# Block 2's experts: all blocks of slots go through one weight piece at a time, with a branch and a load per piece instead of per matrix

## The chip, the cores and the metric

The kernel runs on one core of one Trainium2 chip. The metric is the device time of one launch in microseconds (us). In the profile PE is TensorE's matmuls and PEld its weight loads, DVE is VectorE, ACT is ScalarE, POOL is GpSimd and SP is SyncE, which here only issues transfers; a small q behind a name (PEldq, SPq) means the engine's sequencer, which runs branches, waits and register instructions.

## What is computed

Two blocks of a small network over 512 tokens of 1024 features: attention or recurrence first, then in each block a layer of experts. The change is in the experts of block 2 alone: 32 experts, of which each token goes through 4. From the reference, cut:

```python
def moe_ffn(h, router_w, router_b, w1, b1, w2, b2):
    ...
    logits = (xt @ router_w + router_b).astype(jnp.float32)
    top_val, top_idx = lax.top_k(logits, TOP_K_2)
    gates = jax.nn.softmax(top_val, axis=-1)
    ...
    def run_block(args):
        toks, e = args
        hb = x_pad[toks] @ w1[e] + b1[e]
        g_part = jnp.minimum(hb[..., ::2], SWIGLU_LIMIT)
        u_part = jnp.clip(hb[..., 1::2], -SWIGLU_LIMIT, SWIGLU_LIMIT)
        act = g_part * jax.nn.sigmoid(SWIGLU_ALPHA * g_part) * (u_part + 1)
        return act @ w2[e] + b2[e]
    ...
    out = jnp.zeros((t + 1, shp[-1]), xt.dtype).at[slot_tok].add(y_slots)[:t]
```

w1 of an expert is 1024 x 2048, w2 is 1024 x 1024, in 32-bit floats.

## The kernel before

How many tokens an expert has is only known when the kernel runs; `slots()` works it out and writes it to `cnt`. An expert's slots are cut in four blocks: A is slots 0 to 63, B 64 to 95, C 96 to 127, D 128 to 191. A always runs; B, C and D stand in nested branches on the count n (`If(n > 64)`, `If(n > 96)`, `If(n > 128)`). `ways` says how many column groups of the matmul array a block is spread over: 2 for A and D (matmuls of 64 slots), 4 for B and C (32 slots).

The weights of an expert come in 12 pieces of 1 MB, 8 of w1 and 4 of w2, into a ring of 17 buffers, all by SP's queue in the order of use (`load2w`). A load into a buffer waits until PE has used the piece that was there, and SP issues its loads one after the other.

`moe2` writes the order out by hand (`manual_schedule`). For each expert e: `hidden(e)`, the first product (`hidden2`, matmuls L2637, bias L2642, then on DVE and ACT the activation in L2647 to L2654); `rows(e + 2)`, the gathers of tokens on POOL; the transposes of the next expert's rows, X[e + 1] (L1652); loads; `output(e - 1)`, the second product of the expert before (`output2`, L2668, bias L2671, scaling on DVE into `yy` in L2674, added into the result by a scatter on POOL); loads; the transposes of expert e's result, A[e] (L1652). In `hidden` and `output` there is one `If(n > 64)` each (L2729, L2749); inside, block A's product is done first and then B's, with C and D in nested Ifs (L2731, L2735, L2737 and L2751, L2755, L2757), and an `Else` holds a second copy of block A's product for the experts that have no more. Within a matrix a block goes through all of its pieces before the next block begins, so that the pieces of w1 are let go one by one only during the last block.

The sums of the products lie in PSUM: a pool `ps2` of two pairs of banks for first products, and a pool `ps` of four banks, in turns, for transposes, second products and the matmuls of `slots()`.

Of the kernel before, what the change touches and what calls it, by code (L numbers as in the profile page):

```python
# [85 lines left out]
class Parts:  # L86
    """A float32 operand as the sum of two parts that the tensor engine carries in one pass each."""
# [7 lines left out]
class Pieces:  # L95
    """Blocks in two tiles of four."""
# [7 lines left out]
class Net:  # L104
# [18 lines left out]
    def constants(self):  # L123
# [20 lines left out]
        # additive masks: NEG where the column is before the row / after the row / not after it  # L144
# [9 lines left out]
        # partition numbers  # L154
# [28 lines left out]
    def rsqrt(self, in_, n, scale, eps, name, P=128):  # L183
        """(scale * in_ + eps) ** -0.5 by Newton's method, from the exponent's half."""
# [18 lines left out]
    def vectors(self):  # L203
        """The small vectors: their loads; those of the modulations' inputs as columns; the others."""
# [29 lines left out]
        # silu(c) as padded stationary operands  # L234
# [9 lines left out]
        # biases of the modulations whose vectors are wanted as columns  # L244
# [10 lines left out]
    def parts(self, x, hi, lo):  # L255
        """x as two parts: the rounded one, and what is left."""
# [4 lines left out]
    def mm(self, out, l, r, start, stop):  # L261
        """A matrix product; of operands in parts without the product of their small parts, which are below float32's last place."""
# [7 lines left out]
    def load2(self, src, kk, pool):  # L270
        """A block of weights [kk * 128, 1024 / kk]."""
# [4 lines left out]
    def split2(self, raw, kk, pool=None):  # L276
        """Its parts, in a piece of the ring."""
# [5 lines left out]
    def piece(self, src, ncol, kk=KD, pool=None):  # L283
        """A block of weights [kk * 128, ncol] as [128, kk, ncol]."""
# [12 lines left out]
    def norm_T(self, x, nt, A, B, hT, pool):  # L297
        """hT [128, 8, nt * 128] = (rmsnorm(x) * A + B) transposed."""
# [50 lines left out]
    def projections(self, pace):  # L349
# [3 lines left out]
        # the products by weights: their pieces in the ring, ahead of their parts, ahead of their use  # L353
# [46 lines left out]
        # the first modulation, norm, and what the others want of small inputs  # L400
# [188 lines left out]
    def mods(self, pace):  # L589
        """Both modulations, by two steps a chunk of 512: the first four chunks of each as columns of shifts and of  # L590
        (1 + scale) * norm, the others as a row in DRAM."""
# [11 lines left out]
        for c in range(24):  # L603
# [7 lines left out]
            # partial sums in rows 0, 32, 64, 96 (and 1, 33, ..)  # L611
# [54 lines left out]
    def delta(self, pace):  # L666
        """The gated delta rule, by steps; chunks of a tile of tokens."""
# [9 lines left out]
        # sums of squares of the heads, each in the rows that its factors take  # L677
# [11 lines left out]
        # selectors of the rows of factors, for the channels of a pair of heads  # L689
# [20 lines left out]
        # decays, rates  # L710
# [25 lines left out]
        # factors of q and k in rows: 32 * pair + 10 * part + 2 * kind + head of the pair  # L736
# [30 lines left out]
        # in three bfloat16 parts, which add up to the whole  # L767
# [34 lines left out]
        # token-major: values times rates, keys times decays to the chunk's end  # L802
# [3 lines left out]
        def to_tokens(src, t, fac):  # L806
            # in place: the block of a pair and a tile, channels by tokens, becomes tokens by channels
# [14 lines left out]
        # products of keys and queries within the chunks, with their decays  # L822
# [56 lines left out]
        # inverses of the unit lower triangles: diagonal blocks of 32 by substitution, one per partition  # L879
# [15 lines left out]
        # the transposed inverses take the place of the triangles, block by block; inverses of the blocks of 64, and  # L895
        # the products on the way, side by side
# [69 lines left out]
        # the chunks in turn  # L966
# [61 lines left out]
    def finish(self, pace):  # L1028
        """The outputs of the delta rule's chunks, normed and gated, transposed in the place of the values."""
# [42 lines left out]
    def softplus(self, out, a, b, shape, name):  # L1072
        """out = softplus(a + b)"""
# [9 lines left out]
    def attention(self, pace):  # L1083
        """Sliding-window attention, by steps; its outputs, transposed, in the place of the queries."""
        nc, I, sm, m, t2, ident = self.nc, self.I, self.sm, self.m, self.t2, self.ident
        bank = lambda: self.ps.tile([128, 512], FT, name="ps")
        # rotary angles
# [40 lines left out]
        # norms of the heads: of the queries [tile, 8], of the keys [tile, 2]  # L1128
# [15 lines left out]
        def rope(v, w, r, c, s, shape, ro):  # L1144
            # ro = the rotation of v * w * r by the angles of cosine c and sine s
# [31 lines left out]
        for t in range(NT):  # L1177
            # heads j and j + 4, of the two groups, side by side
# [104 lines left out]
    def out1(self, pace):  # L1283
        """x + gate * (mixed @ w_out) by tiles of tokens, kept in DRAM; by steps."""
# [38 lines left out]
    def norms1(self, pace):  # L1323
        """Norm, modulation and logits of the tiles that out1 is done with."""
# [17 lines left out]
    def norm_tile(self, x, A, B, t, i, h, hT, lg, hold=lambda **n: None):  # L1342
        """rmsnorm(x) * A + B of a tile of tokens: rows to DRAM for the experts; its logits; by steps."""
# [28 lines left out]
    def logits_init(self, pool, parts, n):  # L1372
        """Weights and biases of a router; parts: (w, b, columns)."""
# [11 lines left out]
    def dram_scratch(self):  # L1385
        """Rows of tokens for the experts, what their outputs are added to; spare rows are 512 to 639."""
# [5 lines left out]
        self.xe = [self.dp.tile([S + 128, D], FT, name=f"xe{i}") for i in range(1)]    # outputs of experts in turn in block 1  # L1392
        # numbers of experts, also less 64, halves and quarters
# [16 lines left out]
    def fill_scratch(self, z):  # L1410
        """First contents of the scratch; z: room for 512 words."""
# [9 lines left out]
    def selectors(self):  # L1421
        """Of the heads, by six, in the rows that block 2's decays are made of."""
# [9 lines left out]
    def windows(self):  # L1432
        """One over the sizes of block 2's pooling windows."""
# [10 lines left out]
    def biases(self, src, out):  # L1444
        """The biases of block 2's experts in DRAM as three bfloat16 parts, which add up to the whole."""
# [12 lines left out]
    def argmax(self, l, n, ix, last=False):  # L1458
        """Maximum over the last axis of l [128, 4, n], the one-hot of its first place, and that place less 64 in ix."""
# [29 lines left out]
            # the logits of the chosen group  # L1489
# [19 lines left out]
    def slot_consts(self):  # L1509
        """Numbers of slots, of the spare rows that empty ones take, and of tokens."""  # L1510
# [10 lines left out]
    def slots(self, i, hots):  # L1521
        """Tokens and gates of the first 192 slots of each expert, by blocks of slots; counts per expert."""
# [6 lines left out]
        # ranks of the tokens of an expert, and counts, also as a column  # L1529
# [16 lines left out]
        for k in range(K):  # L1546
# [3 lines left out]
            # the choice's experts times token and gate, and its slots  # L1550
# [24 lines left out]
        # by blocks, each slot as often as its row has pieces  # L1575
# [17 lines left out]
    def table(self, i, K):  # L1593
        """All slots in DRAM: row slot * 32 + expert has the token and its gate."""
# [22 lines left out]
    def mt(self, n, name, bufs):  # L1617
        """Room for n words; within the loop over further slots all pieces take turns in one ring."""
# [1237 lines left out]
```

## Time and profile before

| | us |
|---|---|
| median of 3 runs | 2909.01 |
| runs | 2908.73 to 2913.5 |
| profiled execution, span | 2899.8 |
| PE busy in it | 2242.4 |
| DVE busy in it | 841.4 |

The time of a run is some microseconds longer than the span of a profile, which begins with the first recorded instruction and ends with the last. The experts of block 2 lie in the second half of the span: expert 0's first transposes are at 1594.59 us, and the last product ends at 2870.3 us.

### The profile page before, as it was taken

Reading aid. Unit: us, or ns where it says so; the run is one execution under the profiler, and the core shown is the slowest. Engines: PE = TensorE matmul, PEld = TensorE weight load, DVE = VectorE, ACT = ScalarE, POOL = GpSimd, SP = SyncE. Lnnn points to the kernel's source line nnn. Section 1 sums busy time; section 2 is a strip of 40 time slices with the busy share of each in tenths; the row PEclk is TensorE's granted clock in tenths of the full one; section 3 lists DMA queues with packets and bytes.
Section 4 is the critical chain, followed back from the end, with each engine's and each line's share of the span. In section 5 each row is a group of like instructions: output and inputs, shape, how many; then the busy total and the mean of one; then the engine's idle time right before and its main releaser. Section 6 shows DMA issues by size and latency. Waiting matters only on the chain. (4 is left out here: it accounts for less than half of the span.)

```text
span 2899.8 us, 38736 instructions
## 1 busy us (share of the span) xinstructions
PE 2242.4 (77%) x14872; PEld 1270.8 (44%) x14911; DVE 841.4 (29%) x1743; ACT 551.1 (19%) x1049; POOL 511.7 (18%) x581
## 2 busy tenths in 40 slices
PE   6799698656775538999996877788688787787775
PEld 4566465534544327777685322233223232232222
DVE  3355734311121115666567111110111110110111
ACT  3343311201111016555431000000000000000000
POOL 2333011123331110233214010101101010001000
PEclk9899888678997769999997899899889898898987
DMA  7645424578787743222146988889878689999883
GB/s 266 241 159 176 160 95 167 166 240 260 234 233 247 241 147 92 72 59 65 58 142 228 356 334 334 343 320 361 329 292 313 270 333 358 366 365 366 337 311 103
DMA packets 262355, 691.54 MB, mean 238 GB/s; under 512 B 20199, under 2 KB 135514, under 8 KB 229176
## 3 DMA queue, kind: packets, MB, share of 16 engines
q1 hardware_dynamic: 230936, 614.19, 56.8%
q0 software_dynamic: 26480, 58.03, 7.9%
q10 hardware_dynamic: 4528, 13.63, 1.2%
q8 instruction: 283, 4.64, 0.7%
q14 instruction: 128, 1.05, 0.1%
HBM read 647.23 MB, written 38.57 MB: 237 GB/s over the span
## 5 line engine op out<-in xcount | busy, mean ns | idle before, releaser
L2637 PE MATMUL ps<-w,xT 128*64 128x512 f32 (+1 forms) x3136 | 623.0, 628 | 133.6 <-issue 121.8
L2637 PEld LDWEIGHTS ps<-w,xT 128*64 128x64 f32 (+1 forms) x3136 | 210.3, 136 | 518.0 <-issue 511.7
L2668 PE MATMUL ps<-w,aT 128*64 128x512 f32 (+1 forms) x2048 | 303.3, 507 | 69.4 <-issue 55.8
L1641 POOL DMA_INDIRECT xd<-yy,ix x49 | 77.6, 1583 | 1033.6 <-DVE yy L2674 918.4
L2647 DVE TENSOR_SCALAR gt<-ps 128x512 f32<-128x512 f32 (+1 forms) x49 | 29.6, 604 | 786.3 <-PE ps L2642 761.5
L2668 PEld LDWEIGHTS ps<-w,aT 128*64 128x64 f32 (+1 forms) x2048 | 118.4, 128 | 234.4 <-issue 212.7
L2652 ACT ACTIVATE sg<-gt 128x512 f32<-128x512 f32 (+1 forms) x49 | 27.5, 560 | 765.0 <-DVE gt L2647 765.0
L2674 DVE SCALAR_TENSOR_TENSOR yy<-ps,ga,gate 128x512 f32<-128x512 f32 (+1 forms) x49 | 32.5, 663 | 341.1 <-PE ps L2671 317.4
L1626 POOL DMA_INDIRECT gath<-hd,ix x94 | 93.0, 989 | 179.0 <-issue 46.6
L1667 PE MATMUL ps<-w,xA 128*32 128x128 f32 x1248 | 63.6, 370 | 73.7 <-issue 48.9
L266 PE MATMUL pf<-w,hh 128*128 128x256 f32 (+1 forms) x288 | 100.0, 347 | 2.0 <-ACT hh L257 2.0
L1654 ACT ACTIVATE aT<-ps 128x512 f32<-128x512 f32 (+1 forms) x48 | 24.9, 525 | 392.7 <-PE ps L1652 391.9
L267 PE MATMUL pf<-w,hh 128*128 128x256 f32 (+1 forms) x288 | 93.5, 324 | 0.0
L1667 PEld LDWEIGHTS ps<-w,xA 128*32 128x32 f32 x1248 | 53.6, 151 | 83.9 <-issue 83.2
L1672 DVE TENSOR_TENSOR act<-act,ps 128x64 f32<-128x64 f32 (+1 forms) x45 | 10.4, 230 | 261.0 <-ACT act L1671 236.7
L2019 PE MATMUL pf<-hc,w 128*128 128x256 f32 x256 | 75.8, 447 | 10.0 <-issue 6.0
L266 PE MATMUL pf<-b,b 128*128 128x512 f32 (+2 forms) x224 | 81.1, 362 | 0.0
L266 PE MATMUL pf<-hh,w 128*128 128x512 f32 x192 | 80.4, 419 | 0.0
L268 PE MATMUL pf<-b,b 128*128 128x512 f32 (+2 forms) x224 | 78.1, 349 | 0.5 <-DVE b L258 0.5
L267 PE MATMUL pf<-b,b 128*128 128x512 f32 (+2 forms) x224 | 78.2, 349 | 0.0
L1652 PE MATMUL ps<-ident,gath 128*128 128x128 f32 x266 | 49.3, 300 | 36.5 <-DVE aTA L1689 12.0
L258 DVE TENSOR_TENSOR w<-raw,w 128x1024 fp32r<-128x1024 f32 x52 | 69.0, 1347 | 26.7 <-ACT w L257 26.7
(714 smaller groups left out, 3665.9 us busy)
## 6 DMA issues: line engine op xcount, KB each, us to landing
w<-in_w_dram SPq DMA_DIRECT2D x378, 1024.0 KB
w<-in_w_ada_dram SPq DMA_DIRECT2D x24, 1024.0 KB
w<-in_w_mod_dram SPq DMA_DIRECT2D x24, 1024.0 KB
w<-in_w_down_dram SPq DMA_DIRECT2D x20, 1024.0 KB
w<-in_w_gate_dram SPq DMA_DIRECT2D x37, 512.0 KB
w<-in_w_up_dram SPq DMA_DIRECT2D x37, 512.0 KB
raw<-in_w_in_dram SPq DMA_DIRECT2D x36, 512.0 KB
b<-in_w_gate_dram SPq DMA_DIRECT2D x25, 512.0 KB
```

What stands on the lines that cost most here:

```text
L258: self.nc.vector.tensor_sub(lo, x, hi)
L266: self.nc.tensor.matmul(out, l.hi, r.hi, start=start, stop=False)
L267: self.nc.tensor.matmul(out, l.hi, r.lo, start=False, stop=False)
L268: self.nc.tensor.matmul(out, l.lo, r.hi, start=False, stop=stop)
L1626: nc.gpsimd.indirect_dma_start(out=g, out_offset=None, in_=self.hd[i].rearrange("t (a d) -> (t a) d", a=ways), in_offset=bass.IndirectOffs ...
L1641: self.nc.gpsimd.indirect_dma_start(out=x.rearrange("t (a d) -> (t a) d", a=ways), out_offset=bass.IndirectOffsetOnAxis(ap=ix, axis=0), in ...
L1652: nc.tensor.transpose(p[:, 128 * c:128 * c + 128], g[:, 128 * c:128 * c + 128], self.ident)
L1667: nc.tensor.matmul(p[n * q:n * q + n, 0:2 * f], xT[:, c, n * h:n * h + n], w[:, :, f * q:f * q + f], start=(k == 0), stop=(k == KD - 1))
L2019: nc.tensor.matmul(ps, w[:, k, c0:c0 + 128], hc[:, k], start=(k == 0), stop=(k == KD - 1))
L2637: nc.tensor.matmul(pp[n * j:n * j + n, b], xT[:, c, n * q:n * q + n], w[:, f0:f0 + 512], start=(k == 0), stop=False)
L2668: nc.tensor.matmul(p[n * q:n * q + n, :nd], aT[:, 2 * b + i, n * j:n * j + n], w[:, k % 2, nd * q:nd * q + nd], start=(k == 0), stop=False)
L2674: nc.vector.scalar_tensor_tensor(y, p[:, :nd], ga, self.gates[ways], op0=OP.mult, op1=OP.mult)
```

## The change

`hidden2` and `output2` are cut into a function for one piece of a matrix (`first2`, `second2`) and one for what follows the product (`act2`, `add2`). `hidden(e)` goes over the 8 pieces of w1; at each it runs block A's matmuls and then, in nested branches, those of B, C and D on the same piece, and then SP's load into a buffer is issued (`load`). `output(e)` does the same with the 4 pieces of w2. The `Else` copies are gone. All blocks of an expert are open at once, so the PSUM pools become `ps` with two banks and three named pairs: `h2` for A, `h4` for B and C, `h3` for D. `output` puts the sums of A, B and C into `h3` too, and D's into a bank of `ps`. The transposes of B, C and D move to `inputs` and `results`, with branches of their own, and each of these functions reads the count itself. The loop for more than 192 slots (`further`) uses the new functions, but isn't run with this data.

```diff
-        self.banks("o", 4)
+        self.banks("o", 2, 3)
...
-        def hidden(e):
-            w1 = [W[e, i] for i in range(8)]
-            n = N[e] = nc.values_load(self.cnt[0:1, e:e + 1], engines=self.four, min_val=0, max_val=S)
-            u = U[e] = [self.mt(512, "ut2", 1)]
-            g = G[e]
-            with tc.If(n > 64) as few:
-                x = [self.xpose(g[1], "xT4", 2)]
-                with tc.If(n > 96):
-                    x.append(self.xpose(g[2], "xT4", 2))
-                self.hidden2(X[e], 2, e, w1, 1, u[0])
-                u.append(self.hidden2(x[0], 4, e, w1, 4))
-                with tc.If(n > 96):
-                    u.append(self.hidden2(x[1], 4, e, w1, 4))
-                    with tc.If(n > 128):
-                        self.mp = mq
-                        u.append(self.hidden2(self.xpose(g[3], "xT2"), 2, e, w1, 2))
-            self.mp = mp
-            with few.Else():
-                self.hidden2(X[e], 2, e, w1, 1, u[0])
...
+        def beyond(n, f):
+            with tc.If(n > 64):
+                f(1)
+                with tc.If(n > 96):
+                    f(2)
+                    with tc.If(n > 128):
+                        self.mp = mq
+                        f(3)
+            self.mp = mp
...
+        def inputs(e):
+            X[e] = [self.xpose(G[e][0], "xT2")]
+            beyond(count(e, T.PE, T.Activation), lambda i: X[e].append(self.xpose(G[e][i], ("xT4", "xT4", "xT2")[i - 1], 2 if i < 3 else 1)))
...
+        def hidden(e):
+            n = N[e] = count(e, T.PE)
+            x = X.pop(e)
+            bc = pair("h4")
+            p = [pair("h2"), bc[:, 0:1], bc[:, 1:2], pair("h3")]
+            for k in range(KD):
+                f = lambda i: self.first2(p[i], x[i], ways[i], e, k, W[e, k])
+                f(0)
+                beyond(n, f)
+                load(12 * e + k + 18 - 4 * (e > 0))
+            u = U[e] = [self.act2(p[0], 2, 1)]
+            beyond(count(e, T.DVE, T.Activation), lambda i: u.append(self.act2(p[i], ways[i], 4 if i < 3 else 1)))
+
+        def output(e):
+            n, a = N.pop(e), A.pop(e)
+            U.pop(e)
+            es_ = slice(e, e + 1)
+            o = pair("h3")
+            o3 = self.ps.tile([128, 512], FT, name="ps")
+            p = [o[:, 0], o[:, 1, 0:256], o[:, 1, 256:512], o3]
+            for i in range(4):
+                f = lambda b: self.second2(p[b], a[b], ways[b], e, i, W[e, 8 + i], b != 2)
+                f(0)
+                beyond(n, f)
+                load(12 * e + i + 34)
+            f = lambda b: self.add2(p[b], self.blocks[b][0][:, es_], self.blocks[b][1][:, es_], ways[b])
+            f(0)
+            beyond(count(e, T.DVE, T.Pool), f)
...
```

The order of the instructions shows what this moves on PE. First, two pieces of block A's first product on PE, in the `Else` of L2729 before (`w_` is a buffer of the ring, `xT2` A's transposed rows, DMAHW a load's semaphore):

```order
L2637 MATMUL ps2_21834<-w_21032,xT2_21606 64x512 [waits DMAHW1_49]
L2637 MATMUL ps2_21834<-w_21032,xT2_21606 64x512 x3
L2637 MATMUL ps2_21834<-w_21034,xT2_21606 64x512 [waits DMAHW2_49]
L2637 MATMUL ps2_21834<-w_21034,xT2_21606 64x512 x3
L2637 MATMUL ps2_21834<-w_21036,xT2_21606 64x512 [waits DMAHW4_49]
L2637 MATMUL ps2_21834<-w_21036,xT2_21606 64x512 x3
```

The same place on PE after the change, one piece and the start of the next; the last unconditional branches, with a wait on PE's own semaphore (PE_49), are the arms that run when a block isn't there:

```order
L2634 MATMUL h2_22002<-w_21038,xT2_21920 64x512 [waits DMAHW6_49]
L2634 MATMUL h2_22002<-w_21038,xT2_21920 64x512 x3
L2736 COMPARE_AND_BRANCH
L2634 MATMUL h4_22001<-w_21038,xT4_21937 32x512 [waits DVE_49]
...
L2634 MATMUL h3_22003<-w_21038,xT2_21951 64x512 x3
L2740 UNCONDITIONAL_BRANCH
L2740 UNCONDITIONAL_BRANCH [waits PE_49]
L2738 UNCONDITIONAL_BRANCH [waits PE_49]
L2736 UNCONDITIONAL_BRANCH [waits PE_49]
L2634 MATMUL h2_22002<-w_21359,xT2_21920 64x512 [waits DMAHW7_49]
```

Between two pieces of A there was nothing but the wait for the next load; now there are a branch, the code of three other blocks, and an arm that waits for PE itself.

Second, where the second product of an expert begins on PE, before (in the If; `aT2` is A's transposed result):

```order
L2751 UNCONDITIONAL_BRANCH [waits PE_49]
L2668 MATMUL ps_22243<-w_21618,aT2_21927 64x512 [waits DMAHW4_49,PE_49,Activation_49]
L2668 MATMUL ps_22243<-w_21618,aT2_21927 64x512 x3
L2668 MATMUL ps_22243<-w_21906,aT2_21927 64x512 [waits DMAHW5_49]
L2668 MATMUL ps_22243<-w_21906,aT2_21927 64x512 x3
```

And after:

```order
L2736 UNCONDITIONAL_BRANCH [waits PE_49]
L2671 MATMUL h3_22293<-w_21649,aT2_21958 64x512 [waits DMAHW1_49,DVE_49,PE_49]
L2671 MATMUL h3_22293<-w_21649,aT2_21958 64x512 x3
L2736 COMPARE_AND_BRANCH
L2671 MATMUL h3_22293<-w_21649,aT4_21975 32x256 x8
```

The first matmul waited for the load and for ACT; it now waits for the load and for DVE (DVE_49), since its sums go to the pair h3.

## Rows read from the trace of the kernel before

**Rows 1.** Windows, experts of block 2; columns: busy us by engine, clock, DMA share

```profile
core 0: us, PE busy (x) PEld busy (x) DVE busy (x) ACT busy (x) POOL busy (x), PEclk, DMA share, GB/s
1594.60:2870.40 1275.80, 1010.18 (x5870) 383.09 (x5870) 145.61 (x244) 76.86 (x148) 122.12 (x95) 0.90 0.84 325
2650.00:2700.00 50.00, 33.45 (x148) 12.67 (x148) 5.64 (x9) 3.01 (x6) 6.18 (x5) 0.88 1.00 395
```

**Rows 2.** Waits of PE in 1594.6:2870.4; waiting line, releaser, total us, times, longest

```profile
PE ps L2637 <- issue: 121.8, 20, 7.2
PE ps L2668 <- issue: 55.8, 15, 7.5
PE ps L1652 <- DVE yy L2674: 19.5, 20, 1.0
PE ps L1652 <- PEq L2755: 11.5, 4, 3.3
PE ps L1652 <- ACT sg L2652: 10.0, 9, 1.3
PE ps L2637 <- DMA w<-in_w_dram: 6.7, 1, 6.7
```

**Rows 3.** Single lines' sequencer instructions: count, ns min/median/max, first and last start

```profile
L2729 PEldq COMPARE_BRANCH  x32: 65/6050/6871, 1595.3 to 2815.9; - x32
...
L2751 PEldq COMPARE_BRANCH  x16: 70/202/228, 1647.0 to 2841.0; - x16
...
L2749 ACTq EVENT_SEMAPHORE  x20: 17/17/17, 1689.0 to 2857.9; - x20
...
L2731 PEldq EVENT_SEMAPHORE  x8: 51/51/51, 1596.2 to 2728.9; - x8
...
L2737 PEldq EVENT_SEMAPHORE  x3: 51/51/51, 1962.6 to 2799.3; - x3
...
L2726 PEldq TENSOR_LOAD <-cnt x32: 300/306/321, 1594.6 to 2815.2; - x32
```

**Rows 4.** Timeline of PE; start, us, line, tiles, count, idle time before and releaser

```profile
1711.37 15.80 PE L2637 MATMUL ps<-w,xT 128*64 128x512 f32 x64 [6.32 <-issue]
...
1730.02 7.09 PE L2668 MATMUL ps<-w,aT 128*64 128x512 f32 x32 [0.30 <-PEq L2751]
...
1742.72 0.41 PE L1652 MATMUL ps<-ident,gath 128*128 128x128 f32 x2 [0.33 <-PE ps L1652]
1743.28 13.95 PE L2637 MATMUL ps<-w,xT 128*64 128x512 f32 x64
```

**Rows 5.** Windows behind a gap, and within a first product that has none ahead

```profile
1711.60:1715.00 3.40, 3.40 (x10) 1.04 (x10) 0.00 (x0) 0.00 (x0) 0.00 (x0) 0.50 1.05 390
...
1743.30:1757.20 13.90, 13.90 (x66) 5.65 (x68) 0.00 (x0) 0.31 (x1) 2.59 (x2) 1.00 0.89 332
```

**Rows 6.** PE by line and form in 1594.6:2870.4; busy us, mean ns, idle before

```profile
L2637 PE MATMUL ps<-w,xT 128*64 128x512 f32 x2112 | 509.9, 645 | 133.6 <-issue 121.8 <-DMA w<-in_w_dram 6.7 <-PEq L2731 2.9
L2668 PE MATMUL ps<-w,aT 128*64 128x512 f32 x1024 | 245.1, 634 | 69.4 <-issue 55.8 <-DVE ut L2654 8.5 <-ACT sg L2652 3.4
L2637 PE MATMUL ps<-w,xT 128*32 128x512 f32 x1024 | 113.1, 594 | 0.0
```

**Rows 7.** Timelines of PE and of DVE, between the products of an expert

```profile
1845.66 0.62 PE L2642 MATMUL ps<-b,esel 96*64 96x512 bf16 x4
...
1848.00 7.09 PE L2668 MATMUL ps<-w,aT 128*64 128x512 f32 x32 [1.14 <-issue]
...
1848.60 0.69 DVE L2654 TENSOR_TENSOR ut<-ut,sg 128x512 f32<-128x512 f32 x1
```

**Rows 8.** Timeline of DVE, the last operation on a block B

```profile
1688.47 0.43 DVE L2654 TENSOR_TENSOR ut<-ut,sg 128x256 f32<-128x256 f32 x1
```

**Rows 9.** Timeline of PE, the sums of slots()

```profile
1580.94 7.59 PE L1561 MATMUL ps<-slot,val 128*64 128x192 f32 x32 [0.99 <-DVE slot L1556]
```

**Rows 10.** Waits of SP's queue in 1594.6:2870.4

```profile
SPq L2681 <- PE ps L2637: 345.9, 42, 36.9
```

More of the change, by code (lines that the diff above doesn't have):

```diff
@@ L2622, in route2, with first2, act2 @@
             self.slots(1, hots)
-    def hidden2(self, xT, ways, e, w1, bufs, ut=None):
+    def first2(self, p, xT, ways, e, k, w):
         nc = self.nc
         n = 128 // ways
-        nb = 4 // ways
-        pp = self.ps2.tile([128, 2, 512], FT, name="ps2")
-        for k in range(KD):
-            q, c = divmod(k, 8 // ways)
-            w = w1[k]
-            for b in range(nb):
-                for j in range(ways):
-                    f0 = 512 * (b * ways + j)
-                    nc.tensor.matmul(pp[n * j:n * j + n, b], xT[:, c, n * q:n * q + n], w[:, f0:f0 + 512],
-                                     start=(k == 0), stop=False)
-        for b in range(nb):
+        q, c = divmod(k, 8 // ways)
+        for b in range(4 // ways):
             for j in range(ways):
                 f0 = 512 * (b * ways + j)
-                nc.tensor.matmul(pp[n * j:n * j + n, b], self.esel[:, e:e + 1].to_broadcast([96, n]),
+                nc.tensor.matmul(p[n * j:n * j + n, b], xT[:, c, n * q:n * q + n], w[:, f0:f0 + 512],
+                                 start=(k == 0), stop=False)
+        if k < KD - 1:
+            return
+        for b in range(4 // ways):
+            for j in range(ways):
+                f0 = 512 * (b * ways + j)
+                nc.tensor.matmul(p[n * j:n * j + n, b], self.esel[:, e:e + 1].to_broadcast([96, n]),
                                  self.bp[0][:, f0:f0 + 512], start=False, stop=True)
-        pv = pp[:, 0:nb].rearrange("p b (i c) -> p b i c", c=2)
+    def act2(self, p, ways, bufs, ut=None):
+        nc = self.nc
+        nb = 4 // ways
+        pv = p[:, 0:nb].rearrange("p b (i c) -> p b i c", c=2)
         v = lambda t: t.rearrange("p (b i) -> p b i", b=nb)
@@ L2661, in output2, with add2 @@
         nd = 1024 // ways
-        p = self.ps.tile([128, 512], FT, name="ps")
-        for k in range(KD):
+        for k in (2 * i, 2 * i + 1):
             b, r = divmod(k, 2 * ways)
-            j, i = divmod(r, 2)
-            w = w2[k // 2]
+            j, h = divmod(r, 2)
             for q in range(ways):
-                nc.tensor.matmul(p[n * q:n * q + n, :nd], aT[:, 2 * b + i, n * j:n * j + n],
-                                 w[:, k % 2, nd * q:nd * q + nd], start=(k == 0), stop=False)
+                nc.tensor.matmul(p[n * q:n * q + n], aT[:, 2 * b + h, n * j:n * j + n],
+                                 w[:, k % 2, nd * q:nd * q + nd], start=(k == 0 and clear), stop=False, skip_group_check=True)
+        if i < 3:
+            return
         for q in range(ways):
-            nc.tensor.matmul(p[n * q:n * q + n, :nd], self.esel[:, e:e + 1].to_broadcast([96, n]),
-                             self.bp[1][:, nd * q:nd * q + nd], start=False, stop=True)
-        y = self.mt(nd, f"yy{ways}", ways // 2)
-        nc.vector.scalar_tensor_tensor(y, p[:, :nd], ga, self.gates[ways], op0=OP.mult, op1=OP.mult)
+            nc.tensor.matmul(p[n * q:n * q + n], self.esel[:, e:e + 1].to_broadcast([96, n]),
+                             self.bp[1][:, nd * q:nd * q + nd], start=False, stop=True, skip_group_check=True)
+    def add2(self, p, ix, ga, ways):
+        y = self.mt(1024 // ways, f"yy{ways}", ways // 2)
+        self.nc.vector.scalar_tensor_tensor(y, p, ga, self.gates[ways], op0=OP.mult, op1=OP.mult)
         self.scatter(self.xd[1], y, ix, ways)
@@ L2722, in rows @@
             self.mp = mp
[L2724 to L2736 removed]
+        T = mybir.EngineType
@@ L2737, in hidden, with count @@
+        def beyond(n, f):
+            with tc.If(n > 64):
+                f(1)
+                with tc.If(n > 96):
+                    f(2)
                     with tc.If(n > 128):
                         self.mp = mq
-                        u.append(self.hidden2(self.xpose(g[3], "xT2"), 2, e, w1, 2))
+                        f(3)
             self.mp = mp
-            with few.Else():
-                self.hidden2(X[e], 2, e, w1, 1, u[0])
+        def count(e, *engines):
+            return nc.values_load(self.cnt[0:1, e:e + 1], engines=engines, min_val=0, max_val=S)
@@ new lines, in moe2, with results @@
+        ways = (2, 4, 4, 2)
+        pair = lambda name: self.ps2.tile([128, 2, 512], FT, name=name, bufs=1)
+        def inputs(e):
+            X[e] = [self.xpose(G[e][0], "xT2")]
+            beyond(count(e, T.PE, T.Activation), lambda i: X[e].append(self.xpose(G[e][i], ("xT4", "xT4", "xT2")[i - 1], 2 if i < 3 else 1)))
+        def results(e):
+            A[e] = [self.xpose(U[e][0], "aT2")]
+            beyond(count(e, T.PE, T.Activation), lambda i: A[e].append(self.xpose(U[e][i], ("aT4", "aT4", "aT2")[i - 1], 2 if i < 3 else 1)))
@@ L2744, in output @@
         def output(e):
-            w2 = [W[e, i] for i in range(8, 12)]
+            n, a = N.pop(e), A.pop(e)
+            U.pop(e)
             es_ = slice(e, e + 1)
-            n, u = N[e], U[e]
-            out = lambda a, ix, ga, ways: self.output2(a, ix[:, es_], ga[:, es_], ways, e, w2)
-            with tc.If(n > 64) as few:
-                a = [self.xpose(u[1], "aT4", 2)]
-                with tc.If(n > 96):
-                    a.append(self.xpose(u[2], "aT4", 2))
-                out(A[e], ixA, gaA, 2)
-                out(a[0], ixB, gaB, 4)
-                with tc.If(n > 96):
-                    out(a[1], ixC, gaC, 4)
-                    with tc.If(n > 128):
-                        self.mp = mq
-                        out(self.xpose(u[3], "xT2"), ixD, gaD, 2)
@@ L2760, in output @@
-            self.mp = mp
-            with few.Else():
-                out(A[e], ixA, gaA, 2)
+            o = pair("h3")
[7 more added lines that the diff above has]
+            f = lambda b: self.add2(p[b], self.blocks[b][0][:, es_], self.blocks[b][1][:, es_], ways[b])
@@ L2788, in block @@
             x = self.xpose(self.gather(1, ix, 2), None)
-            self.output2(self.xpose(self.hidden2(x, 2, e, w[0], 1), None), ix, ga, 2, e, w[1])
+            p = pair("h2")
+            for k in range(KD):
+                self.first2(p, x, 2, e, k, w[0][k])
+            a = self.xpose(self.act2(p, 2, 1), None)
+            p = pair("h3")[:, 0]
+            for i in range(4):
+                self.second2(p, a, 2, e, i, w[1][i])
+            self.add2(p, ix, ga, 2)
         self.further(1, self.modr[:, 7168:8192], weights, block)
```

10 lines of the change are left out of this document (4 added, 6 removed).

## The prediction

> **What bounds the kernel now.** I read the windows of the experts of block 2 first. From 1594.6 us, the first transposes of expert 0, to 2870.4 us, the end of the last product, the program spends 1275.8 of its 2899.8 us; PE is busy for 1010.2 of them, DVE for 145.6, and the DMA engines move 415 MB at a share of 0.84 [rows 1]. A 50 us window in which they are full (share 1.00) moves 395 GB/s; at that rate 415 MB would take 1050 us, so the loads are near but are not the limit over the stretch. The chain is PE's: its 265.6 us of idle time are what a change of order can win.
>
> The waits of PE name that time [rows 2]: 121.8 us in 20 gaps before L2637, the first product, and 55.8 before L2668, the second, wait for nothing that the profile shows ("issue"); 11.5 us stand on PE's own sequencer at L2755. One gap of 6.7 us is put down to a load, but is of the same length and place, and I count it with them. What they are is told by the instructions of PE's sequencer [rows 3]: COMPARE_BRANCH on L2729 takes 65 ns at least, 6050 ns in the median and 6871 at most, and that on L2751, whose jump goes over two transposes only, 202 ns. L2729 jumps over all of the code of blocks A to D, to the copy of block A in the Else. 20 experts take it (the false arm of L2749 is run 20 times by ACT), 8 stop behind B (L2731's, on PE) and 3 behind C (L2737's); so one runs A to D. The far jumps cost 121.8 + 55.8 + 11.5 + 6.7 = 196 us.
>
> They cost a second time. At 1711.37 us a first product starts behind such a gap of 6.32 us, and its 64 matmuls take 15.80 us; where no gap is ahead they take 13.95 [rows 4]. [...] From the groups by form [rows 6]: 33 full-size first products took 509.9 us, at 13.95 they would take 460.4; 32 second products took 245.1, at the 7.09 of the row at 1730.02 they would take 226.9; the matmuls of the quarter blocks, which have no such gap ahead, lie at 594 ns each, against 645 for those. That is 49.5 + 18.2 = 68 us of slow matmuls. Without both PE would need 1275.8 - 196 - 68 = 1012 us.
>
> **The change part by part.** *Gone: the far jumps and the slow clock behind them, -196 and -68 us.* The new jumps go over B, C and D of one piece, 58 instructions by the order, and end in or next to the code at hand; L2751's 202 ns is their row, and that lies under matmuls already issued.
>
> *Added: an end at each piece.* The order shows it: behind a piece's matmuls the false arm waits for PE's own semaphore, that is, for the piece's last matmul, before the next piece's first is issued. 12 pieces x 32 experts = 384, less the 12 of the one expert that runs all four blocks. Before, such an arm stands at one If or two of an expert: two transposes end at 1742.72 + 0.41 = 1743.13, the first matmul starts at 1743.28, 0.15 us idle [rows 4]. A piece also loses its overlap: one matmul lasts 0.594 us [rows 6], while pairs follow each other every 13.95 / 32 = 0.436 us, so 0.16 us more. That makes 0.31; I take 0.35 for the 20 x 12 pieces of experts with A alone. Where the arm is reached from inside (B or C ran), one more branch stands ahead; the gap at 1730.02 is 0.30, others of this kind 0.55, with the overlap 0.46 to 0.71; I take 0.65 for 11 x 12 pieces. 84 + 86 = +170 us. Bounds: 0.15 for each, the overlap kept, is 56; 0.71 for each is 264. No gain is possible here.
>
> [...]
>
> *Moved: where the second product of expert e-1 begins.* It now writes the pair h3, which block D of expert e's first product also has; so its first matmul waits for DVE's false arm, behind the last operation on expert e's result. In an expert with A alone, the first product ends at 1845.66 + 0.62 = 1846.28, the second began at 1848.00, 1.72 later, while DVE finished at 1848.60 + 0.69 = 1849.29 [rows 7]; with 0.25 for arm and branch, 1.5 us later than now. In experts with B, act2 of B comes behind that of A with four operations of 0.42 [rows 8] while PE has only one piece of B left to do: about 2 us, 2.5 with C. 20 x 1.4 + 8 x 2 + 4 x 2.5 = +54, say +55 us; bounds 30 and 80 (nothing else is ready on PE then; queued behind are all of e-1's matmuls and A[e]'s transposes, and SP's loads of the pieces that they free). The gap is then about 2.5 us; +5 for a slow clock behind some.
>
> *Smaller.* The transposes of A[e] no longer wait for the yy of e-1 (19.5 us in 20 waits [rows 2]); PE instead reads the count three times per expert rather than once, 306 ns and the register operations each [rows 3], of which one lies under the new wait: equal, bounds -20 and +30. The transposes of u[1] leave their place before the second product: -10, the row on sg [rows 2]. Code: PE now walks through all of it in about 31 us instead of jumping; I allow 0.6 us per expert with A alone, +12, bounds 0 and 20. ps has two buffers instead of four, so slots() has its matmuls of L1561 (at 1580.94 [rows 9]) wait for cnt and most, some 2.4 us of DVE work: +2.
>
> *Loads.* A load is issued as soon as its piece is free, not at the end of a matrix or an If. SP waited 345.9 us on L2637 in 42 times [rows 10]; but of PE's longest waits only the one of 6.7 us is put down to a load, so this adds nothing. It must only hold: an expert with A alone, without gap and slow clock, is 13.95 + 2.34 + 7.09 us to the end of its second product [rows 4, 7], with what stands between that and the next about 25; after the change about 25 + 12 x 0.35 + 1.4 + 0.6 = 31. Its 12 pieces and rows, a 32nd of 415 MB, need 33 us at 395 GB/s. A ring of 17 pieces and the heavier experts between carry such a run.
>
> Sum: -196 - 68 + 170 + 55 + 5 + 12 + 2 - 10 = -30 us. From a span of 2899.8 to 2870; the median, 2909.0, lies 9.2 above the span, so 2879.
>
> **The rivals.**
> - *Ends of pieces cheap.* For it: the wait is one instruction of 51 ns, and sequencer and matmuls overlap elsewhere. Against it: the 0.15 us at 1743.13. At 0.15 each: -114 more, 2765; at 0.31 each 2824. [...] Chance 0.20.
> - *Ends of pieces dear, slower than before.* The weights of the next piece's matmul, its semaphore and the branch start only behind the wait. The 0.55 us at other Ifs speaks for it. At 0.71 each, +94: 2973. It decides from a mean of (170 + 30) / 372 = 0.54 us per piece; I have 0.46. [...] Chance 0.23.
> - *A draw:* the price per piece near 0.54, 2903 to 2915 (0.2%, about what this measurement can tell). Chance 0.10.
> - *Loads take over:* the A-alone experts fall to 33 us each: +2 x 20 = 40, less what the ring holds, 2890 to 2915. The unfilled share (0.84) speaks against it. Chance 0.05, a third of it a draw.
>
> **The numbers.** The forecast, 2840 to 2903, has 0.42. Faster: 0.42 + 0.20 + 0.03 and a little of the cases near the edge, 0.66; same 0.11; slower 0.23. Range 2800 to 2935: it leaves out the cheapest ends and the dearest, 0.2 together. For a faster outcome alone it is 2800 to 2903.
>
> **What would show it.** No COMPARE_BRANCH of 6 us on PE; clock 1.00 over most of the stretch; a gap of 0.15 us behind every eight matmuls of L2634, released by PE itself; the second product starting about 0.3 us behind DVE's last operation; SP's loads one at a time. The forecast is wrong if the time for a piece of A in a first product is far from 1.74 + 0.35 = 2.09 us, if 6 us gaps remain, or if PE waits for loads.

## The result, and the profile after

The changed kernel is slower: 2952.7 us in the median (2936 to 2960 in 4 runs) against 2908.9 (2908 to 2914), a ratio of 1.0126, 95% interval 1.009 to 1.0162. Forecast was 2879, with a range of 2800 to 2935. Its profiled execution has a span of 2947.7 us, 47.9 more than before. Its runs differ more than those of the kernel before, and they go with the clock granted over the whole run: 0.909 in the shortest, 0.896 in the longest.

The experts' window, in the columns of [rows 1], from the first transposes to the end of the last product:

```profile
1598.40:2912.40 1314.00, 1087.67 (x5870) 328.07 (x5870) 144.88 (x244) 78.67 (x148) 120.48 (x94) 0.95 0.85 315
```

It is 38 us longer than 1275.8. PE's idle time fell from 265.6 to 226.3 us, but its busy time rose by 77.5 with the same 5870 matmuls. The waits of PE in it, with the columns of [rows 2]:

```profile
PE h L2671 <- DVEq L2736: 39.3, 19, 3.3
PE h L2634 <- PEq L2738: 27.2, 57, 1.1
PE h L2634 <- PEq L2736: 22.7, 35, 1.3
PE h L2634 <- issue: 14.0, 13, 1.3
PE h L2671 <- DVEq L2738: 11.5, 5, 2.5
```

The 121.8 and 55.8 us of "issue" are gone. In their place stand DVE's false arms ahead of the second product (L2671), and PE's own arms ahead of the first and between its pieces (L2634). The branches answer to L2729 in [rows 3]; the register load to L2726:

```profile
L2736 PEldq COMPARE_BRANCH  x448: 65/208/2192, 1599.1 to 2910.2; - x150
...
L2746 PEldq TENSOR_LOAD <-cnt x96: 297/305/322, 1598.4 to 2902.3; - x96
```

The median branch takes 208 ns and none takes 6 us: the far jumps are gone. (Twelve take 1.1 to 2.2 us, but PE's matmuls run on through all but 0.3 us of them.) The count is read 96 times instead of 32. The timeline of PE through an expert with A alone shows the price of an end, as in [rows 4]:

```profile
2383.43 0.63 PE L1652 MATMUL ps<-ident,gath 128*128 128x128 f32 x4 [0.30 <-PEq L2736]
2386.64 1.94 PE L2671 MATMUL h<-w,aT 128*64 128x512 f32 x8 [2.58 <-DVEq L2736]
...
2395.36 0.63 PE L1652 MATMUL ps<-ident,ut 128*128 128x128 f32 x4 [0.30 <-PEq L2736]
2397.22 1.94 PE L2634 MATMUL h<-w,xT 128*64 128x512 f32 x8 [1.23 <-PEq L2736]
2399.31 1.94 PE L2634 MATMUL h<-w,xT 128*64 128x512 f32 x8 [0.15 <-PEq L2736]
...
2428.07 1.94 PE L2634 MATMUL h<-w,xT 128*64 128x512 f32 x8 [1.23 <-PEq L2736]
```

A piece of A starts every 2399.31 - 2397.22 = 2.09 us: 1.94 of work, 0.15 idle. That is the 1.74 + 0.35 of the forecast. And an expert with A alone, when the clock stays high, takes 2428.07 - 2397.22 = 30.85 us; 31 was forecast. So the loss isn't there. In an expert with B a piece of the first product starts every 3.39 us (1679.28 - 1675.89), 0.76 more than its matmuls take without ends (13.95 / 8 + 7.07 / 8 = 2.63; 7.07 is the 113.1 us of [rows 6] over 16 products of a quarter block):

```profile
1675.89 2.93 PE L2634 MATMUL h<-w,xT 128*64 128x512 f32 x16 [1.25 <-issue]
1679.28 2.93 PE L2634 MATMUL h<-w,xT 128*64 128x512 f32 x16 [0.46 <-PEq L2738]
```

What stayed is the slow clock. Around one fall, in the timeline of PE and then in windows (the last numbers are clock, DMA share and GB/s, as in [rows 5]):

```profile
1706.91 1.94 PE L2671 MATMUL h<-w,aT 128*64 128x512 f32 x8 [2.47 <-DVEq L2738]
...
1715.63 0.63 PE L1652 MATMUL ps<-ident,ut 128*128 128x128 f32 x4 [0.30 <-PEq L2736]
1717.00 0.44 PE L1652 MATMUL ps<-ident,ut 128*128 128x128 f32 x2 [0.75 <-ACT aT L1654]
1718.55 5.56 PE L2634 MATMUL h<-w,xT 128*64 128x512 f32 x16 [1.11 <-issue]
```

```profile
1715.40:1718.50 3.10, 1.06 (x6) 0.62 (x6) 0.75 (x1) 0.98 (x2) 1.62 (x1) 1.00 0.89 304
1719.20:1722.60 3.40, 3.25 (x9) 0.58 (x6) 0.00 (x0) 0.00 (x0) 0.42 (x1) 0.50 1.03 366
```

Between the second product and the next first product PE works 1.06 of 3.1 us, in small pieces between waits of 0.3 to 1.1 us. Then the granted clock is 0.50, and two pieces take 5.56 us instead of 2 x 2.09. No gap of 6 us stands ahead of it.

The gaps of PE, added up by what stands before and behind them, and the clock's records (which clock was granted from when to when) laid over the matmuls, give the whole difference of the two profiled executions (us). A stretch at 0.50 counts as lost by half of the time that matmuls run in it, an estimate: after the change 9 matmuls lie in the 3.40 us at 0.50 from 1719.2, and 16 in the 3.30 us at 1.00 from 1722.7.

| | before | after | change | forecast |
|---|---|---|---|---|
| idle before a first product | 130.0 | 36.8 | -93 | -128 |
| idle before a second product | 69.9 | 61.3 | -9 | -1 |
| idle at the transposes | 61.7 | 43.2 | -18 | -22 |
| idle within and between products | 3.9 | 85.0 | +81 | |
| PE's busy time if the clock were full | 940.0 | 1028.3 | +88 | |
| these two, the ends of the pieces | | | +169 | +170 |
| lost to the slow clock | 70.2 | 59.3 | -11 | -63 |
| code, as an own term | | | 0 | +12 |
| start of the experts (slots) | 1594.6 | 1598.4 | +4 | +2 |
| from the last product to the end | 29.4 | 35.3 | +6 | 0 |
| sum | | | +48 | -30 |

Before, 260 us at 0.50 held 140 us of matmuls: half of the slow time fell into gaps in which there was nothing to slow down. After, 131 us hold 119 us of matmuls.

### The profile page after: what moved, and what is told of

It reads as the page before. It is cut to its first block, busy times and chain, and to the rows that moved or that the text cites. A ratio compares the mean times of both kernels' runs of the same rounds, so it can differ in the third digit from the quotient of the medians.

```text
span 2947.7 us, 40372 instructions
## 1 busy us (share of the span) xinstructions
PE 2323.8 (79%) x14911; PEld 1204.3 (41%) x14911; DVE 837.3 (28%) x1743; ACT 553.0 (19%) x1049; POOL 510.9 (17%) x581
## 5 line engine op out<-in xcount | busy, mean ns | idle before, releaser
L2634 PE MATMUL h<-w,xT 128*64 128x512 f32 (+1 forms) x3136 | 657.8, 619 | 94.0 <-PEq L2738 27.2
L2671 PE MATMUL h<-w,aT 128*32 128x256 f32 (+1 forms) x2048 | 343.9, 531 | 89.1 <-DVEq L2736 39.3
L2634 PEld LDWEIGHTS h<-w,xT 128*64 128x64 f32 (+1 forms) x3136 | 169.2, 129 | 554.6 <-issue 547.2
L2651 DVE TENSOR_SCALAR gt<-h 128x512 f32<-128x512 f32 (+1 forms) x49 | 29.6, 604 | 766.7 <-PE h L2641 765.4
L2671 PEld LDWEIGHTS h<-w,aT 128*32 128x32 f32 (+1 forms) x2048 | 104.9, 129 | 309.3 <-issue 292.8
L2682 DVE SCALAR_TENSOR_TENSOR yy<-h,ga,gate 128x512 f32<-128x512 f32 (+1 forms) x48 | 31.5, 661 | 399.4 <-PEq L2736 197.7
L2019 PE MATMUL pf<-hc,w 128*128 128x256 f32 x256 | 69.7, 419 | 10.0 <-issue 6.0
L1310 PE MATMUL pf<-w,b 128*128 128x512 f32 x128 | 69.9, 697 | 8.2 <-DMA w<-in_w_out_dram 8.2
```

The source lines that it names most:

```text
L1310: nc.tensor.matmul(p, src[:, k], W[half, n][:, k], start=(k == 0), stop=(k == 3))
L2019: nc.tensor.matmul(ps, w[:, k, c0:c0 + 128], hc[:, k], start=(k == 0), stop=(k == KD - 1))
L2634: nc.tensor.matmul(p[n * j:n * j + n, b], xT[:, c, n * q:n * q + n], w[:, f0:f0 + 512], start=(k == 0), stop=False)
L2671: nc.tensor.matmul(p[n * q:n * q + n], aT[:, 2 * b + h, n * j:n * j + n], w[:, k % 2, nd * q:nd * q + nd], start=(k == 0 and clear), stop= ...
L2682: self.nc.vector.scalar_tensor_tensor(y, p, ga, self.gates[ways], op0=OP.mult, op1=OP.mult)
```

## The experiments

The runs took place on three chips on which the kernel before had medians of 2906, 2916 and 2906 us, so that ratios to it (with 95% intervals) are compared; the changed kernel is at 1.0126. The expectations were written as times from its 2953 us, so they are compared by the distance from it.

**The theory after the result:** the ends cost what was forecast; the change loses because the clock falls as often as before, where PE is thinly used ahead of each product, and because PE reads the count three times. **Rivals:** the ends are dearer than the trace shows; the loads set the pace.

**fill: work in the gap ahead of the second product.**

```diff
-        for c in range(n):
+        for c in list(range(n)) * again:
...
-            X[e] = [self.xpose(G[e][0], "xT2")]
+            X[e] = [self.xpose(G[e][0], "xT2", 1, 4)]
```

> The four transposes of the next expert's rows are written four times over, the same values into the same bank: 12 more transposes, some 2 us of PE work per expert, in the time in which PE waits for DVE. Nothing else changes. Theory 1 (the clock falls because PE is thinly used there): the clock stays high more often, the work is free; 2953 - 15 to 40 = 2913 to 2938, mean clock in the experts above 0.95. Rival (the clock does not depend on that stretch, or costs nothing): 2953 to 2975, clock 0.95 as it was.

Measured: 2917.3 us, ratio 1.0038 (1.0017 to 1.0058): some 26 us faster than the changed kernel, with 384 matmuls more; 15 to 40 were expected by theory 1. Its window and the same place in its timeline as above:

```profile
1603.50:2879.30 1275.80, 1083.61 (x6254) 363.80 (x6254) 144.97 (x244) 78.80 (x148) 120.20 (x94) 0.99 0.87 325
```

```profile
1709.31 1.94 PE L1652 MATMUL ps<-ident,gath 128*128 128x128 f32 x16 [0.54 <-ACT sg L2656]
1712.40 1.94 PE L2671 MATMUL h<-w,aT 128*64 128x512 f32 x8 [1.16 <-DVEq L2738]
...
1724.33 1.94 PE L2634 MATMUL h<-w,xT 128*64 128x512 f32 x8 [1.11 <-issue]
1726.42 1.94 PE L2634 MATMUL h<-w,xT 128*64 128x512 f32 x8 [0.15 <-PEq L2736]
```

The wait on DVE is 1.16 instead of 2.47 us, filled with useless work, and the mean clock is 0.99. By the clock's records 14.6 us are lost instead of 59.3. A second product that starts at the low clock in the changed kernel, and the same one with the fill:

```profile
1860.07 0.63 PE L1652 MATMUL ps<-ident,gath 128*128 128x128 f32 x4 [0.30 <-PEq L2736]
1863.25 3.28 PE L2671 MATMUL h<-w,aT 128*64 128x512 f32 x8 [2.55 <-DVEq L2736]
```

```profile
1862.60:1865.90 3.30, 2.65 (x8) 0.85 (x8) 0.01 (x1) 0.00 (x0) 0.00 (x0) 0.50 1.02 407
```

```profile
1861.30 1.94 PE L1652 MATMUL ps<-ident,gath 128*128 128x128 f32 x16 [0.30 <-PEq L2736]
1864.50 1.94 PE L2671 MATMUL h<-w,aT 128*64 128x512 f32 x8 [1.26 <-DVEq L2736]
```

The place of the falls tells which stretch they belong to; each fall that begins in the window of the experts is counted for the product that starts or runs behind it:

| falls of the clock ahead of | a first product | a second product |
|---|---|---|
| before | 21 | 9 |
| after | 12 | 19 |
| fill | 7 | 0 |
| one_count | 1 | 13 |
| own_bank | 9 | 17 |
| two_pieces | 7 | 20 |

With 1.94 us of transposes in the gap instead of 0.63, none of the 19 falls ahead of a second product is left: they go with the little work that PE has there. Whether the 2.5 us without work count or the small pieces around them, the run doesn't tell, as it changes both. But at 11 of the 12 falls ahead of a first product in the changed kernel, PE has had no gap over 1.3 us since the second product before it began (the twelfth is in expert 1, with no second product before it), so these 11 came without a long gap. That stretch is as thin with the fill as without it and keeps 7 of its 12 falls; why five went, the one shown above among them, is not shown.

**one_count: the count read once per engine, in `inputs`.**

```diff
-            beyond(count(e, T.PE, T.Activation), lambda i: X[e].append(...
+            N[e] = nc.values_load(self.cnt[0:1, e:e + 1], engines=self.four, min_val=0, max_val=S)
+            beyond(N[e], lambda i: X[e].append(...
...
-            n = N[e] = count(e, T.PE)
+            n = N[e]
```

> The count of an expert is read once per engine (in inputs) instead of three times on PE. Theory 1: the idle time between A's transposes and the first product, 36.8 us in 32 gaps of 1.15, falls to some 0.3 each, 27 us less, and slow periods that begin there get fewer: 2905 to 2925. Rival (the register loads run ahead of the engine and lie under the transposes): no more than 5 us, 2945 to 2955.

Measured: 2893.4 us, ratio 0.9955 (0.9939 to 0.9972), some 50 us faster than the changed kernel (28 to 48 were expected) and faster than the one before. The place between A's transposes and the first product, in its timeline:

```profile
2370.13 0.63 PE L1652 MATMUL ps<-ident,ut 128*128 128x128 f32 x4 [0.57 <-PEq L2736]
2370.91 1.94 PE L2634 MATMUL h<-w,xT 128*64 128x512 f32 x8
```

The 36.8 us before a first product are 8.3, though the transposes now wait 28.0 + 24.6 us instead of 11.9 + 11.7, which takes 18 of these 28 us back. The idle time before a second product fell too, from 61.3 to 42.2 us: DVE's read of the count, which stood ahead of its false arm, went as well. In all 29 us of idle time went. The falls ahead of a first product went from 12 to 1 and the loss to the clock from 59.3 to 26.5. The clock gave as much as the idle time; the rival, that the register loads lie under other work, falls.

**two_pieces: a branch and its loads per two pieces.**

```diff
-            for k in range(KD):
-                f = lambda i: self.first2(p[i], x[i], ways[i], e, k, W[e, k])
+            for k in range(0, KD, 2):
+                def f(i):
+                    for j in range(k, k + 2):
+                        self.first2(p[i], x[i], ways[i], e, j, W[e, j])
```

> A branch per two pieces instead of per piece: 186 ends instead of 372, and loads issued when two pieces are done. If an end costs what the trace shows (0.35 us in experts with A alone, 0.76 in others, 184 us in all), half of it goes: 2953 - 92 = 2861, less if the longer jumps leave the code at hand (6 us each would be seen as branches of 6 us on L2736). If the ends are dearer than that and are the whole of the loss, 2820 to 2840. If they are cheap and lie beside other waits, 2930 to 2950.

Measured: 2832.0 us, ratio 0.9748 (0.971 to 0.9786), some 110 us faster than the changed kernel. By its time it lies between the price from the trace (92) and the rival of dearer ends (113 to 133). The trace shows 49 us less idle time within products, 50 us less busy time at full clock, 11 less to the clock. So the 186 ends that went were worth 99 us, 0.53 each, and the 186 that stay cost the other 70 of the 169, 0.38 each: an end cost more in the kernel with more of them, which is not explained here. The 0.76 us of pieces in experts with B is no price for all of their ends either: with 0.35 for the others it would make 184 us instead of 169.

**own_bank: A's second product in the bank of ps.**

```diff
-            p = [o[:, 0], o[:, 1, 0:256], o[:, 1, 256:512], o3]
+            p = [o3, o[:, 1, 0:256], o[:, 1, 256:512], o[:, 0]]
```

> Block A's second product gets the bank of ps and D's the bank of h3, so that the second product of an expert no longer waits for DVE's false arm. The changed kernel stood at 2953 us (median). Theory 1 (the slow clock came back: PE is idle or thinly used between the products of each expert, and the granted clock falls there once per expert): the 61 us of idle time before L2671 fall to some 15, and the slow periods that begin there go; 2953 - 46 - 20 to 30 = 2875 to 2890. Rival (the ends of the pieces are what costs, the clock follows anything): only the wait itself goes, 2900 to 2915, with as many slow periods as before. Rival 2 (the loads became the limit): the time saved is waited for at the weights, 2930 to 2953.

Measured: 2923.3 us, ratio 1.006 (1.0037 to 1.0083), some 19 us faster, much less than theory 1 (63 to 78) and its first rival (38 to 53) expected. That is in the range of the second rival, the loads, but not for its reason: none of PE's waits of 8 us or more in total is for weights (1.1 us in the changed kernel). The wait on DVE had a second one right behind it, as the waits of PE and a timeline of ACT show:

```profile
PE ps L2671 <- ACTq L2736: 36.9, 20, 3.0
```

```profile
1863.85 0.63 ACT L2656 ACTIVATE sg<-gt 128x512 f32<-128x512 f32 x1 [18.32 <-DVE gt L2651]
1864.65 0.60 ACT L1654 ACTIVATE xT<-ps 128x512 f32<-128x512 f32 x1 [0.17 <-ACTq L2736]
```

`ps` has two banks; the one for the second product was last used for transposed rows, whose copy stands on ACT behind the sigmoid, its arm and the copy of A's rows. Idle time before a second product fell only from 61.3 to 46.9, and the clock fell nearly as often (17 instead of 19).

**hidden_only: the first product by pieces, the second per matrix with an `Else`, as before.** `output` is that of the kernel before, with the transposes left in `results`.

> One part of the change alone: the first product goes through the pieces one at a time, the second product is done per matrix as before, with an If, an Else copy of block A and sums in ps. If the first product's part is where the time went (its 256 pieces hold two thirds of the ends, and the counts on PE stay three), it is slower than the kernel before by about what its ends cost less the far jumps at the first product: 128 us of jumps gone, 8/12 of 170 = 113 us of ends, 35 us at the start of each first product, the slow clock kept by the jumps that stay at L2749: 2909 + 10 to 45 = 2920 to 2955. Rival (the second product's wait on DVE is what costs, and its removal here wins): 2860 to 2890.

Measured: 2998.8 us, ratio 1.0288 (1.0254 to 1.0322), slower than both and than expected. The branch at the second product's If (L2749 before, 65 ns to 7790, median 848), and the wait before the second product:

```profile
L2797 PEldq COMPARE_BRANCH  x32: 65/2657/6250, 1659.0 to 2949.2; - x32
```

```profile
PE ps L2696 <- issue: 100.3, 18, 7.0
```

Its far jumps cost more than before: 100.3 us of "issue" in 18 waits against 55.8 in 15 [rows 2]. The branches aren't longer: added up they take 90 us against 87, but before PE's matmuls ran on through 33 us of them, and now through almost none. So the half with the far jumps lost more by the change of the other half. The window of the experts is 88 us longer than before: 127 for the ends of the first product (61 idle, 66 busy; 113 were expected), 56 more idle time before a second product, 90 less before a first, and a small rest; the slow clock took 69 us as before.

**half_loads: every second piece of weights not loaded.**

```diff
-            q = j % 17
+            if j % 2:
+                self.W2[self.todo2[j]] = self.W2[self.todo2[j - 1]]
+                continue
+            q = j // 2 % 17
```

> The changed kernel with every second piece of weights left out: the odd pieces are not loaded, and the products use the even piece before instead, so the sums are other ones; the instructions of PE and their branches are the same. If the loads cost the changed kernel anything, it gets faster by that much: the rival says 2900 to 2930 against 2953. Theory 1 (ends of pieces, idle time at the counts and the slow clock, none of them the loads): 2940 to 2960.

Measured: 2943.9 us, ratio 1.0124 (1.0097 to 1.0152), the changed kernel's own. The DMA share went from 0.85 to 0.48 and the window stayed:

```profile
1598.20:2909.00 1310.80, 1085.28 (x5870) 328.12 (x5870) 144.96 (x244) 78.53 (x148) 119.85 (x93) 0.95 0.48 160
```

What the loads cost the changed kernel is less than the intervals can tell, some 10 us, and the window is 3 us shorter. This rival falls.

**Combinations.** Two pieces per branch with one count (two_count), with the bank as well (all3), and with four pieces per branch (all3_four); then `fill` on the last two, with the transposes written twice instead of four times (all3_fill, four_fill), and all3 with half of the loads.

> Two pieces per branch and one read of the count per engine. Both alone took 121 and 60 us from 2953. If the two are separate causes the sum holds: 2953 - 181 = 2772 (2760 to 2785). If the count's gain is mostly the granted clock that comes back, and the clock depends on the place between the products alone, the same sum. Rival (the loads become the limit: 415 MB at 395 GB/s take 1050 us, against some 1130 that would be left): 2800 to 2820, PE waits for weights.

> Two pieces per branch, one count, and block A's second product in a bank of ps. In the run with that bank alone L2671 waited for ACT's arm instead of DVE's, 46.9 us instead of 61.3, so the bank is worth 10 to 25 us at most here too: 2750 to 2770. Rival (with the count read early the arms are through sooner and the bank no longer matters): as without it, within 5 us.

> As the one with all three, but four pieces per branch: 93 ends instead of 186, and jumps twice as long over B, C and D. If jumps cost only when their target is not at hand and four pieces still fit, another 45 us go: 2710. If they do not fit, branches of up to 6 us on PE appear, at most 60 in the 20 experts with A alone, and the slow clock behind them: 2800 to 3000.

> The same on the kernel with two pieces per branch, one count and the bank of ps (2775). Its DMA engines are at a share of 0.97 in the experts, so here the loads may set the pace: PE's waits name no weights, but a bound by the loads would give 2720 to 2750 without half of them. If PE is still the chain, 2765 to 2780.

> The same with two pieces per branch (2775 without it, 22 us lost to the slow clock): 2760 to 2770 by the theory of thin use, 2775 to 2790 by the rival.

> Four pieces per branch, one count, the bank of ps, and the transposes of the next expert's rows written twice (0.65 us of PE work more per expert, in idle time). The profiled run without that lost 44 us to the slow clock and had 31 us of idle time at that place. If thin use of PE there makes the clock fall, some 20 to 30 us come back: 2740 to 2750. If not, 2770 to 2780.

| | us | ratio to before | interval | lost to the clock in the profiled run, us |
|---|---|---|---|---|
| two_count | 2795.7 | 0.9575 | 0.9544 to 0.9606 | 35.6 |
| all3 | 2775.3 | 0.9520 | 0.9494 to 0.9545 | 22.1 |
| all3_four | 2769.7 | 0.9496 | 0.9466 to 0.9526 | 44.4 |
| all3_half | 2754.7 | 0.9483 | 0.9444 to 0.9522 | 20.8 |
| all3_fill | 2763.3 | 0.9510 | 0.9485 to 0.9534 | 8.2 |
| four_fill | 2746.7 | 0.9460 | 0.9429 to 0.9492 | 23.6 |

Pieces and count add up: -3.8 and -1.7 of a hundred apart, -5.5 together, against a changed kernel at +1.3. (In us that is 160, a little short of the 168 to 193 expected, which took differences of medians from two chips.) The bank gives about half of a hundredth more here (16 us; 10 to 25 were expected), though the two intervals just touch. Four pieces save another 24 us of work at full clock (952.6 against 976.8) and 18 us of idle time within products, but give 22 back to the clock and 16 at the transposes, so that neither expectation held. The first branches of 6 us are there again, 6.09 at most against 3.76 in all3; 16 on this line take over 3 us, against 2 in all3, though matmuls run on through most of that time:

```profile
L2736 PEldq COMPARE_BRANCH  x223: 65/208/6087, 1609.2 to 2735.5; - x112
```

Half of the loads change all3 by less than the intervals can tell (11 us, at the edge of what was expected if PE sets the pace), although its DMA engines were at a share of 0.95; whether the loads cost all3 a little is open. The filling takes about half of the loss to the clock away (44.4 to 23.6) or more (22.1 to 8.2), but its gain in time is within the intervals (10 and 3 us; 20 to 30 and 5 to 15 were expected). four_fill has the lowest time; against all3_four and all3_half it isn't told apart. All of those that compute the whole result beat the kernel before by 4 to 5%.

## Why the prediction was wrong

**The step that failed** is "Gone: the far jumps and the slow clock behind them, -196 and -68 us". The jumps went; the clock did not come back: 59 of 70 us stayed. The prediction took the slow clock, 0.50 right behind the gap [rows 5], for a follower of a 6 us gap, though it had itself put a gap of 2.5 us ahead of each second product, and allowed 5 us there. 52 of the 78 us between forecast and result in the profiled execution are this, and fill shows where the falls come from. None of the three signs of being wrong that it named came: a piece of A took 2.09 us, no gap of 6 us was left, and PE waited for weights 1.1 us in all. The clock, which decided, was not among them.

**Right:** the ends of the pieces, +169 against +170, with A alone 0.35 each and in experts with B 0.76 rather than 0.65 in the first product, so that the sum is closer than its parts, which is in part luck; the time of an expert with A alone, 30.85 against 31 (with luck too: 0.6 us for code that didn't come, and nothing for the count); the second product's wait, which it put at +55 against the 56 us of jumps that it replaces; the short jumps, 208 ns in the median, 2.2 us at most, none of 6 us. What these runs show is how long a branch took; which code is at hand, and why a far jump takes 6 us, no run shows.

**Mis-sized:** the count. The prediction set two more register loads against the end of the wait on yy, "equal". The wait on yy did go, but the loads of A's transposes and of the first product come one behind the other with a branch and an arm between: 36.8 us in 32 gaps where the jumps apart there had been almost none, +35. one_count shows that it is theirs, and that the one read that is left still costs something at the transposes. The code term of +12 was the author's allowance, and no run shows it: in the changed kernel no branch on L2736 takes more than 2.2 us, and no gap of its own stands for it.

**Not seen:** 6 us at the end. All blocks' second products now end together, and their scatters queue on POOL; two of these three rows name the landing of the one before as what ended the wait:

```profile
2909.42 1.56 POOL L1641 DMA_INDIRECT xd<-yy,ix  x1 [4.93 <-DMA xd<-yy,ix]
2913.99 1.56 POOL L1641 DMA_INDIRECT xd<-yy,ix  x1 [3.01 <-DVEq L2736]
2918.65 1.57 POOL L1641 DMA_INDIRECT xd<-yy,ix  x1 [3.10 <-DMA xd<-yy,ix]
```

Before, expert 30's three scatters were under way while its later blocks were still computed, so the last expert's could start 1 us after its product. Now it starts 6.3 us after 2912.4.

**The rivals.** The dear ends, on the slower side, forecast 2973: the sign was theirs, the mechanism wasn't; the ends cost 0.45 on average, not 0.54 or more. The cheap ends and the loads were wrong, the latter by half_loads.

## What to carry to other kernels

In this kernel the loss to the slow clock was not tied to the gap behind which it was found: if the change leaves PE thinly used at the same beat, book the loss as kept until a trace shows otherwise (59 of 70 us stayed when the gaps of 6 us were gone). Here an end of a branch in the loop, the wait for PE's own last matmul and the lost overlap, cost 0.35 us per piece with A alone and 0.45 in the mean, so the size of what one branch covers was the number to tune: one piece lost 1.3%, two won 2.5% alone, and with four, branches of up to 6.09 us were there again and 38 of the 42 us that the fewer ends saved went to the clock and the transposes. Read a count once and keep it (50 us here); when a wait is taken away, look which one stands right behind it (behind DVE's here 36.9 us on ACT).

## What the runs showed of the hardware that was not expected

Adding 1.3 us (1.94 - 0.63) of useless matmuls per expert made the kernel 26 us faster: the mean granted clock over the experts was 0.99 instead of 0.95, and 14.6 us were lost to the slow clock instead of 59.3. And of the far branches PE lost what its matmuls didn't cover: the 32 branches at the second product's If take 87 us before, 33 of them under running matmuls, and 90 in hidden_only, almost none of it under matmuls; PE's gaps of "issue" ahead of the second product were 55.8 and 100.3 us.
